# Splitting four of W_out's eight row blocks in the second half's narrow projection groups, and loading them as parts at attention's end

## The chip, the cores and the metric

One core of one Trainium2 chip runs the kernel. The metric is device time in microseconds (us). The kernel has engines with queues of their own, each of which runs its instructions in order: TensorE (PE; its weight loads are listed as PEld), VectorE (DVE), ScalarE (ACT), GpSimd (POOL) and SyncE (SP). SP does no arithmetic and issues most DMA transfers; POOL and ACT can issue DMAs too. Sixteen DMA engines serve all queues.

## The reference

One decoder layer on 2048 tokens of width 1024, in float32: an RMSNorm, one input projection, two mixers (gated linear attention, GLA, and dilated sliding-window attention), an output projection, then an MLP. What matters here is the output projection, which takes the GLA heads' 512 columns (after their own norm, with its gain `gla_norm_g`) and the attention heads' 512 columns through one matrix of 1024 x 1024:

```python
o_a = o_a * lax.rsqrt(jnp.mean(o_a * o_a, axis=-1, keepdims=True) + EPS)
o_a = o_a * gla_norm_g[l].astype(jnp.float32).reshape(GLA_HEADS, GLA_DV)
o_a = o_a.reshape(B, S, GLA_WIDTH) * jax.nn.silu(gr.astype(jnp.float32))
...
mixed = jnp.concatenate([o_a, o_b], axis=-1).astype(h.dtype)
h = h + jnp.einsum('bsm,md->bsd', mixed, w_out[l])
```

## The kernel before

A product in float32 precision is made of three TensorE products of parts (`mm3`, L139 to L142): each operand is *split* into a rounded part hi, which ScalarE writes, and the rest lo, which VectorE writes. So every matrix that takes part has to be split somewhere, at a cost of one ScalarE and one VectorE operation for each piece.

The kernel runs in stages: the input projection (to about 476 us), attention with GLA beside it (to about 855 us), the output projection W_out with the norm (to about 1035 us), then the MLP.

*Input projection.* The tokens are taken in two halves, and in each half nine groups of W_in's columns are gone through (`groups`), numbered g = 0 to 8 and, in the second half, NG = 9 to 17. A group has seven jobs (`jobs`), the seven products of a Strassen-like scheme. The *narrow* groups, g = 11 to 16 in the second half, have 128 columns; their jobs have the order 1, 2, 6, 5, 7, 3, 4 (`linked`), and each is twelve products of 128x512, some 2.7 us. `prep(at + 2)` splits the weights of the job after next (ScalarE L304, VectorE L306, or L308 where a scale goes in) and adds them up in place (VectorE L310 to L316). `load_w` fetches the next group's raw weights (`wraw`), on SP's queue, or on POOL's for the last group. L310 is the first operation that needs a group's new weights. The order of instructions written out in this part ends with the first half. From there on a planner, at compile time, gives each engine its order from a model of the costs; `tc.keep_in_program_order` pins one instruction behind all that its engine was given so far.

*SBUF.* All large tiles come from one ring of 25 slots (`slot`, L127). A tile that wants a slot waits until an earlier tile is done with, and a DMA into it waits on its queue.

*Attention.* The loop goes by units of score blocks: scores (L930, L932), VectorE's bias and minimum (L940), ScalarE's exponential (L941), transposes (L950), the copy of the transposed block to `pt` by ScalarE (L957) or VectorE (L959) in turns, products with v (L969). GLA's steps run between them (L1093 to L1165; L1107 copies the scores under a mask, L1160 needs what it copied, L1153 is an exponential). Other work is hung on unit numbers by `at_unit`. One such work is `load_wo`: in the last units, every third unit, one of W_out's eight rows of blocks c (128 rows each) is loaded whole, 0.5 MB, into `woraw` (SP, L1188). Rows 0 to 3, GLA's, are multiplied by the norm's gain `gn` and split into the blocks 1 (left half) and 12 (right half), in tiles `wb` (ScalarE L1193, VectorE L1194). Rows 4 to 7 are split whole into tiles `wo` (L543, L544, in the helper `split`). The rows go in the order 4, 0, 1, 5, 2, 3, 6, 7. Each `wb` tile holds two rows' pieces of one block, hi and lo.

*Output projection.* It reads the parts by `wo_part`, the first products after 853 us. Further blocks (4 to 7) are sums of these; their sums were made earlier in attention by `sum_wo` on POOL, stored to `wtD`, and are loaded and split by `mix_wo`.

The main lines of `load_wo`:

```python
c = (4, 0, 1, 5, 2, 3, 6, 7)[len(loaded)]
...
raw = slot("woraw")[:, :D]
SP.dma_start(raw, wo[:, c])
```

Of the kernel before, what the change touches and what calls it, by code (L numbers as in the profile page):

```python
# [18 lines left out]
D = 1024  # L19
# [10 lines left out]
AHEAD, LAG = 3, 2  # L30
# [84 lines left out]
def emit(tc, a, stop=99):  # L115
    nc = tc.nc
    V, A, G, T, SP = nc.vector, nc.scalar, nc.gpsimd, nc.tensor, nc.sync
# [4 lines left out]
    dram = es.enter_context(tc.tile_pool(name="dram", bufs=1, space=bass.MemoryType.DRAM))  # L122

    def ps(tag):
        return psum.tile([128, 512], F32, name="ps_" + tag, tag=tag, bufs=BANKS[tag])

    def slot(name, dt=F32, n=SLOT):  # L127

        return up.tile([128, SLOT], dt, name=name, tag="u", bufs=25)[:, :n]

    def view(t, shape):
        n = int(np.prod(shape))
        names = "abcd"[:len(shape)]
        return t[:, :n].rearrange(f"p ({' '.join(names)}) -> p {' '.join(names)}", **dict(zip(names, shape)))
# [27 lines left out]
    gn = stats[:, 44:]  # L162
    stat_at = [0]

    def stat(n=1):
        if stat_at[0] + n > 44:
            stat_at[0] = 0
        s = stats[:, stat_at[0]:stat_at[0] + n]
        stat_at[0] += n
        return s  # L170

    def rstd_of(ssq, width, n=1, bias=eps):
        r = stat(n)
        A.activation(r, ssq, AF.Ln, bias=bias, scale=1.0 / width)
        A.activation(r, r, AF.Exp, scale=-0.5)
        return r
# [75 lines left out]
    NG = len(groups)  # L252
# [3 lines left out]
    jobs = [(g, j) for g in range(2 * NG) for j in (linked if chained(g) else order)]  # L256
# [263 lines left out]
    def bias_rows():  # L520

        rb, oh, rbo = xp[:33, :8], view(xp[:33, 8:], (3, 384)), view(bp[:8], (3, 384))
        SP.dma_start(rb[:32], a["rel_bias"])
        SP.dma_start(oh, a["c_onehot"])
        V.memset(rb[32:33], NEG)
        yield
        V.tensor_scalar(rb[:32], rb[:32], -1.0, None, op0=OP.mult)
        for d in range(3):
            p = ps("d")
            T.matmul(p[:8, :384], rb, oh[:, d], start=True, stop=True)  # L530
            V.tensor_copy(rbo[:, d], p[:8, :384])
        SP.dma_start(rowD, rbo)
        yield
# [8 lines left out]
    def split(hi, lo, src):  # L542
        A.activation(hi, src, AF.Copy)  # L543
        V.tensor_tensor(lo, src, hi.bitcast(F32), op=OP.subtract)  # L544

    def x_load(t, dst):
        SP.dma_start(dst, x2[t * 128:t * 128 + 128])
# [13 lines left out]
    def transposed(xt, last=None, pin=False, by=ident):  # L561
        out = []
        for q in range(2):
            pv = view(ps("cd"[q]), (4, 128))
            for k in range(4):
                of = xt[:, (4 * q + k) * 128:(4 * q + k + 1) * 128]
                ins = T.transpose(pv[:, k, :], last if last is not None and 4 * q + k == 7 else of, by)
                if pin and q + k == 0:
                    tc.keep_in_program_order(ins)
            out.append(pv)  # L570
        return out
# [33 lines left out]
    def second_half():  # L605

        b = [view(bp[:, 512 * q:], (4, 128)) for q in range(4)]
        for i in range(4):
            for k in range(2):
                x_load(8 + 4 * k + i, xp[:, D * k:D * k + D])  # L610
            yield
            for k in range(2):
                xt = xp[:, D * k:D * k + D]
                ss = stat()
                tc.keep_in_program_order(A.activation(bp[:, :D], xt, AF.Square, accum_out=ss))
                r = rstd_of(ss, D)
                V.scalar_tensor_tensor(xt, xt, r, gB, op0=OP.mult, op1=OP.mult)
            yield
            for k in range(2):
                for q, pv in enumerate(transposed(xp[:, D * k:], pin=True, by=perm)):  # L620
                    A.activation(b[2 * k + q], pv, AF.Copy)
                yield
            (b11, b21, b12, b22), (t2, t4, t3) = b, [view(xp[:, 512 * q:], (4, 128)) for q in range(3)]
            V.tensor_tensor(b12, b12, b11, op=OP.subtract)
            V.tensor_tensor(t2, b22, b12, op=OP.subtract)
            for j, v in ((2, b21), (1, b11), (5, b12), (6, t2), (3, b22), (4, t4), (7, t3)):
                if j == 5:
                    yield
                    V.tensor_tensor(t4, b21, t2, op=OP.subtract)
                    V.tensor_tensor(t3, t2, b11, op=OP.subtract)  # L630
                SP.dma_start(nTD[j - 1][:, :, i * 128:i * 128 + 128], v)
            yield
# [21 lines left out]
    def reload(n):  # L654

        j, cs = order[n // 2], slice(1024 * (n % 2), 1024 * (n % 2) + 1024)
        t = (xp, bp)[n // 2 % 2][:, cs]
        SP.dma_start(t, nTD[j - 1].rearrange("p c s -> p (c s)")[:, cs])

        def rest():  # L660
            hi, lo = [v[:, cs] for v in TF[j]]
            tc.keep_in_program_order(A.activation(hi, t, AF.Copy))
            V.tensor_tensor(lo, t, hi.bitcast(F32), op=OP.subtract)
            if n + 4 < 14:
                back.append(reload(n + 4))

        return rest

    with tc.manual_schedule(engines={nc.tensor.engine, nc.vector.engine, nc.scalar.engine, nc.gpsimd.engine}):
# [19 lines left out]
        w = view(first_w[0][0], (2, 4, 256))  # L689
# [108 lines left out]
    SP.dma_start(w2b[33:50].bitcast(F32), w2raw[33:].bitcast(F32))  # L798
    for gT in gTs:
        A.activation(gT, ident, AF.Copy, scale=0.0)  # L800
    other, back, bias = second_half(), [], bias_rows()
    for at in range(7, len(jobs)):
        g = jobs[at][0]
        prep(at + 2)
        if at in (7 * NG - 7, 7 * NG - 6):
            back.extend(reload(2 * (at - 7 * NG + 7) + k) for k in range(2))
        for i in range(4 if groups[g % NG][2] > 128 else 1):
            ready = gated[:]
            product(at, i)()
            for t in ready:  # L810
                gate_product(t)
                gated.remove(t)
        if behind and chained(g):
            f, *args = behind.pop(0)
            f(*args)
        if back and at >= 7 * NG - 5:
            back.pop(0)()
            back.pop(0)()
        if at in OTHER:
            next(other)  # L820
        if at == len(jobs) - 14:
            heads = load_head(0)
        if at in (len(jobs) - 13, len(jobs) - 10, len(jobs) - 9):
            next(heads)
        if at in (7 * NG + 3, 7 * NG + 5):
            next(bias)
        if 7 * NG + 8 <= at < 7 * NG + 44 and at % 3 == 0:
            spread_bias(2 - (at - 7 * NG - 8) // 12, (at - 7 * NG - 8) // 3 % 4 * 2)
# [336 lines left out]
                    A.activation(st[:, j], st[:, j], AF.Copy, scale=w[:, j:j + 1])  # L1165
                yield

    wo = a["w_out"].rearrange("o (c p) n -> p (o c) n", p=128)
    WO, WB, loaded = {}, {}, []

    def block_view(j, c):

        if (j, c // 2) not in WB:
            WB[j, c // 2] = view(slot(f"wb{j}", FR), (2, 2, 512))
        return [WB[j, c // 2][:, c % 2, i] for i in range(2)]

    def wo_part(j, c):

        if j in (2, 3):
            return [WO[c][:, i, 512 * (j - 2):512 * (j - 2) + 512] for i in range(2)]  # L1180
        return block_view(j, c)

    def load_wo(n):
        for _ in range(n):
            c = (4, 0, 1, 5, 2, 3, 6, 7)[len(loaded)]
            loaded.append(c)
            raw = slot("woraw")[:, :D]
            SP.dma_start(raw, wo[:, c])  # L1188
            if c < 4:
                for j, n in ((1, 0), (12, 1)):  # L1190
                    hi, lo = block_view(j, c)
                    r = raw[:, 512 * n:512 * n + 512]
                    A.activation(hi, r, AF.Copy, scale=gn[:, c:c + 1])  # L1193
                    V.scalar_tensor_tensor(lo, r, gn[:, c:c + 1], hi.bitcast(F32), op0=OP.mult, op1=OP.subtract)  # L1194
            else:
                w = WO[c - 4] = view(slot("wo", FR), (2, D))
                split(w[:, 0], w[:, 1], raw)

    wtD = dram.tile([4, 128, 2 * D], F32, name="wtD")

# [56 lines left out]
    def at_unit(n, *f):  # L1257
        plan.setdefault(n, []).append(f)
# [16 lines left out]
    for pr in range(4):  # L1275
# [3 lines left out]
        for hh, br in seq:  # L1279
# [7 lines left out]
            if br == 2 and first:  # L1287
                pieces = load_head(b.h)
# [15 lines left out]
    NU = len(units)  # L1304
# [1 line left out]
    for n, x in enumerate(sums_wo):  # L1306
        at_unit(8 + AHEAD + n, next, x)
    for i in range(8):
        at_unit(NU - 28 + 3 * i + AHEAD, load_wo, 1)
    gla = gla_steps()  # L1310
    for k in range(-AHEAD, NU + LAG):
        tr, pv, sc = iter(()), iter(()), iter(())
# [314 lines left out]
    for at in range(4):  # L1627
        p, e = divmod(at, 2)
# [31 lines left out]
    for g in range(14, 56):  # L1660
        p, i = divmod(g, 7)
# [161 lines left out]
    for at in range(len(jobs1)):  # L1823
# [7 lines left out]
        n = at + 6 - len(jobs1)  # L1831
# [15 lines left out]
    for ph, (_, chained, _, _) in enumerate(PRODUCTS):  # L1847
# [3 lines left out]
        for k in range(4):  # L1851
            n = 4 * ph + k
# [76 lines left out]
```

## Time and profile before

| | us |
|---|---|
| median of 3 runs | 2239.28 |
| lowest and highest | 2235.93, 2239.9 |
| the profiled execution | 2235.3 |
| its span, first to last instruction | 2233.5 |
| share of PE, DVE, ACT, POOL busy in the span | 99%, 74%, 55%, 24% |

How to read the lines that follow. A row of the *timeline* has the start and the length in us, the engine, the line of the code, the operation, what it writes <- what it reads, the shape, and in brackets the idle time of the engine before it with what ended that. A row of the *waits* names who waited <- for what: us in total, times, longest. A row of the *groups* ends with: busy time, mean ns of one | idle time before, with what ended most of it. A row of the *DMA issues* has how many, KB each, and the median us from issue to landing. A row of the *windows* gives a stretch of time, its length, then the busy time (and instructions) of PE, PEld, DVE, ACT and POOL, the clock that TensorE was granted (1.00 is full speed), the busy share of the DMA engines, and GB/s. DMA times are on SP's queue where a row says SPq. A matmul's end is modelled, so TensorE's busy time isn't the same as TensorE at its peak.

### The profile page before, as it was taken

To read this page: it belongs to the slowest core of one execution; us is meant where nothing else is said; L and a number is where in the kernel's file an instruction comes from. 1 tells how busy PE (TensorE), PEld (TensorE's weight loads), DVE (VectorE), ACT (ScalarE), POOL (GpSimd) and SP (SyncE) were. 2 spreads that over 40 slices of the span, in tenths; PEclk is the share of its full clock that TensorE was granted. 3 is DMA by queue.
4 is the path that set the end of the run, shared out by engine and by line. 5 is a ranking of instruction groups with operands and counts; after the bars stand their busy time and mean duration, and the time that the engine had idled before them with its cause. 6 is when DMAs were issued, how large, how long until landed. Compare 5 with 4: busy or idle time off the path is not lost.

```text
span 2233.5 us, 34965 instructions
## 1 busy us (share of the span) xinstructions
PE 2208.3 (99%) x12420; PEld 1918.8 (86%) x12420; DVE 1650.9 (74%) x3093; ACT 1236.2 (55%) x2420; POOL 528.4 (24%) x527
## 2 busy tenths in 40 slices
PE   9999999999999999999999999999999999999998
PEld 8988998899999988887788887888888888888877
DVE  8676766657777788778776788777686697576798
ACT  7365524437888885546555566555555433333446
POOL 1000000026586673000000000000007222042462
PEclk9999999999999999999999999999999999999999
DMA  6566855677967966768644456555489998677775
GB/s 208 176 216 190 268 152 170 208 216 260 322 226 238 278 199 245 239 227 269 208 147 142 140 178 192 158 174 161 130 287 284 307 295 270 216 247 253 253 258 197
DMA packets 331763, 491.50 MB, mean 220 GB/s; under 512 B 20615, under 2 KB 225050, under 8 KB 320836
## 3 DMA queue, kind: packets, MB, share of 16 engines
q1 hardware_dynamic: 307282, 381.97, 52.7%
q0 software_dynamic: 16960, 54.60, 9.7%
q10 hardware_dynamic: 7346, 52.70, 6.2%
q8 instruction: 98, 1.61, 0.3%
q14 instruction: 77, 0.63, 0.1%
HBM read 335.25 MB, written 158.66 MB: 221 GB/s over the span
## 4 chain that ended last, share of the span: by engine, by line
PE 75%; issue 16%; DMA 3%; DVE 3%; POOL 2%; ACT 1%; POOLq 0%; ACTq 0%; SPq 0%; DVEq 0%
PE ps_a L141 8%; PE ps_a L142 8%; PE ps_a L140 8%; PE ps_c L141 6%; PE ps_c L142 6%; PE ps_c L140 6%; PE ps_a L969 4%; PE ps_d L141 4%; PE ps_d L142 4%; PE ps_d L140 4%; PE ps_o L140 3%; PE ps_o L141 3%; PE ps_o L142 3%; PE ps_d L950 3%; PE ps_c L932 2%
## 5 line engine op out<-in xcount | busy, mean ns | idle before, releaser
L543 ACT ACTIVATE cb<-bs 128x1024 fp32r<-128x1024 f32 x104 | 110.1, 1060 | 286.4 <-PE ps_c L141 95.4
L544 DVE TENSOR_TENSOR cb<-bs,cb 128x1024 fp32r<-128x1024 f32 x104 | 161.5, 1553 | 136.8 <-ACT cb L543 136.4
L1749 POOL TENSOR_TENSOR bs<-bs,rb 128x1024 f32<-128x1024 f32 x60 | 173.9, 2904 | 312.8 <-DMA bs<-w_ff 280.8
L544 DVE TENSOR_TENSOR w1comb<-w1raw,w1comb 128x512 fp32r<-128x512 f32 x224 | 153.5, 687 | 92.5 <-ACT w1comb L543 92.4
L1456 POOL DMA_DIRECT2D w1raw<-w_ff x64 | 48.1, 752 | 701.4 <-DVE w1comb L544 524.9
L543 ACT ACTIVATE w1comb<-w1raw 128x512 fp32r<-128x512 f32 x224 | 139.8, 627 | 89.1 <-PE ps_c L142 26.1
L969 PE MATMUL ps_a<-v,pt 128*128 128x65 f32 x1200 | 178.6, 253 | 1.8 <-ACT pt L957 1.8
L969 PEld LDWEIGHTS ps_a<-v,pt 128*128 128x128 f32 x1200 | 173.9, 195 | 3.8 <-ACT pt L957 2.7
L941 ACT ACTIVATE pe<-pe,O 128x256 f32<-128x256 f32 (+1 forms) x384 | 154.9, 453 | 13.5 <-DVE O L940 12.3
L950 PE MATMUL ps_d<-ident,pe 128*128 128x128 f32 x600 | 159.5, 280 | 1.2 <-ACT pt L957 1.1
L304 ACT ACTIVATE wcomb<-wraw 128x512 fp32r<-128x512 f32 (+2 forms) x119 | 90.4, 759 | 114.4 <-PE ps_a L141 54.6
L940 DVE CUSTOM_DVE_ANT_0 pe<-ps_c,nb 128x256 f32<-128x256 f32 (+1 forms) x384 | 125.7, 360 | 34.3 <-PE ps_d L950 23.0
L140 PE MATMUL ps_c<-hb,w1comb 128*128 128x512 f32 x320 | 124.6, 390 | 0.8 <-DVE acc L1545 0.8
L141 PE MATMUL ps_c<-hb,w1comb 128*128 128x512 f32 x320 | 124.5, 389 | 0.0
L142 PE MATMUL ps_c<-hb,w1comb 128*128 128x512 f32 x320 | 124.0, 389 | 0.0
L141 PE MATMUL ps_c<-cb,ca 128*128 128x512 f32 x312 | 121.4, 389 | 0.0
L142 PE MATMUL ps_c<-cb,ca 128*128 128x512 f32 x312 | 121.4, 389 | 0.0
L140 PE MATMUL ps_c<-cb,ca 128*128 128x512 f32 x312 | 121.4, 389 | 0.0
L544 DVE TENSOR_TENSOR ca<-ra,ca 128x1024 fp32r<-128x1024 f32 x84 | 119.7, 1426 | 0.1
L306 DVE TENSOR_TENSOR wcomb<-wraw,wcomb 128x512 fp32r<-128x512 f32 (+2 forms) x77 | 73.2, 950 | 53.3 <-ACT wcomb L304 53.2
L950 PEld LDWEIGHTS ps_d<-ident,pe 128*128 128x128 f32 x600 | 108.6, 186 | 1.7 <-ACT pt L957 1.3
L1530 ACT ACTIVATE acc<-acc 128x512 f32<-128x512 f32 x96 | 60.6, 632 | 68.3 <-DVE acc L1549 31.7
(490 smaller groups left out, 7174.4 us busy)
## 6 DMA issues: line engine op xcount, KB each, us to landing
ra<-actD ACTq DMA_DIRECT2D x50, 1024.0 KB, 7.4
actD<-ring SPq DMA_DIRECT2D x176, 256.0 KB, 3.0
rb<-w_ff SPq DMA_DIRECT2D x88, 512.0 KB, 5.9
bs<-w_ff SPq DMA_DIRECT2D x72, 512.0 KB, 6.6
w1raw<-w_ff POOLq DMA_DIRECT2D x64, 512.0 KB, 5.5
k<-kD SPq DMA_DIRECT2D x16, 1024.0 KB, 9.0
rb<-hTD SPq DMA_DIRECT2D x28, 512.0 KB, 5.0
wraw<-w_in SPq DMA_DIRECT2D x48, 256.0 KB, 3.7
```

The lines of the kernel that those rows point to most:

```text
L140: T.matmul(out, sh, mh, start=first, stop=False, **kw)
L141: T.matmul(out, sl, mh, start=False, stop=False, **kw)
L142: T.matmul(out, sh, ml, start=False, stop=last, **kw)
L304: A.activation(hi, src, AF.Copy, scale=sc)
L306: V.tensor_tensor(lo, src, hi.bitcast(F32), op=OP.subtract)
L543: A.activation(hi, src, AF.Copy)
L544: V.tensor_tensor(lo, src, hi.bitcast(F32), op=OP.subtract)
L940: V.tensor_tensor_reduce(p, s, bias, scale=1.0, scalar=BIG, op0=OP.add, op1=OP.min, accum_out=nm)
L941: A.activation(p, p, AF.Exp, bias=nm, scale=-1.0)
L950: T.transpose(pb[:, i * 128:i * 128 + 128], src, ident)
L969: T.matmul(self.b.opsum[:, n % 4], self.pt[:, i * 128:i * 128 + 128], self.b.v[:, blk, cols], start=first, stop=last)
L1749: (engines or ((G,), (V, V))[len(sums) - 1])[e].tensor_tensor(v, v, r, op=OP.add if op == "+" else OP.subtract)
```

## The change

Rows 0 to 3 of W_out are no longer loaded and split at attention's end. In the second half of the input projection a new generator, `split_wo`, takes two slots (`wsum` for two raw rows, `wsplit` for parts). At the job with index 4 of group 11 POOL issues the loads of rows 0 and 1. After job 6 (the third job) of each of the groups 12 to 15 one row is taken: two ScalarE operations (hi, with the gain), two VectorE operations (lo) and, on POOL's queue, two stores of 0.5 MB to the new DRAM tiles `wsD`, for block 1 and for block 12; after rows 0 and 1 POOL also loads rows 2 and 3. At attention's end the places of rows 0 to 3 in `load_wo` are taken by four loads of ready parts (`load_parts`), 1 MB each, straight into `wb` tiles on SP's queue: (block 1, rows 0 and 1), (block 12, rows 0 and 1), and the same with rows 2 and 3. Rows 4 to 7 are loaded and split as before, and all eight places keep their units.

```diff
+    wo = a["w_out"].rearrange("o (c p) n -> p (o c) n", p=128)
+    wsD = {j: dram.tile([2, 128, 2, 2, 512], F32, name=f"wsD{j}") for j in (1, 12)}
+
+    def split_wo():
+
+        raw, pieces = view(slot("wsum"), (2, D)), view(slot("wsplit", FR), (2, 2, 512))
+        for c in range(2):
+            G.dma_start(raw[:, c], wo[:, c])
+        yield
+        for n in range(8):
+            c, h = divmod(n, 2)
+            p = pieces[:, h]
+            r = raw[:, c % 2, 512 * h:512 * h + 512]
+            w = gn[:, c:c + 1] if c < 4 else 1.0
+            tc.keep_in_program_order(A.activation(p[:, 0], r, AF.Copy, scale=w))
+            V.scalar_tensor_tensor(p[:, 1], r, w, p[:, 0].bitcast(F32), op0=OP.mult, op1=OP.subtract)
+            G.dma_start(wsD[((1, 12), (2, 3))[c // 4][h]][c % 4 // 2, :, c % 2], p.bitcast(F32))
+            if h and c < 2:
+                G.dma_start(raw[:, c % 2], wo[:, c + 2])
+            yield
+
+    of_wo = split_wo()
...
+        if at == 7 * NG + 18:
+            next(of_wo)
+        if NG + 3 <= g < NG + 7 and jobs[at][1] in (6,):
+            for _ in range(2):
+                next(of_wo)
...
+    def load_parts(j, h):
+
+        t = slot(f"wb{j}", FR, 2048)
+        WB[j, h] = view(t, (2, 2, 512))
+        SP.dma_start(t.bitcast(F32), wsD[j][h].rearrange("p c i n -> p (c i n)"))
+
...
-    def load_wo(n):
-        for _ in range(n):
-            c = (4, 0, 1, 5, 2, 3, 6, 7)[len(loaded)]
-            loaded.append(c)
+    def load_wo(c):
+        if isinstance(c, tuple):
+            load_parts(*c)
+        else:
             raw = slot("woraw")[:, :D]
             SP.dma_start(raw, wo[:, c])
-            if c < 4:
-                for j, n in ((1, 0), (12, 1)):
-                    hi, lo = block_view(j, c)
-                    r = raw[:, 512 * n:512 * n + 512]
-                    A.activation(hi, r, AF.Copy, scale=gn[:, c:c + 1])
-                    V.scalar_tensor_tensor(lo, r, gn[:, c:c + 1], hi.bitcast(F32), op0=OP.mult, op1=OP.subtract)
-            else:
-                w = WO[c - 4] = view(slot("wo", FR), (2, D))
-                split(w[:, 0], w[:, 1], raw)
+            w = WO[c - 4] = view(slot("wo", FR), (2, D))
+            split(w[:, 0], w[:, 1], raw)
...
-        at_unit(NU - 28 + 3 * i + AHEAD, load_wo, 1)
+        at_unit(NU - 28 + 3 * i + AHEAD, load_wo, (4, (1, 0), (12, 0), 5, (1, 1), (12, 1), 6, 7)[i])
```

More of the change, by code (lines that the diff above doesn't have):

```diff
@@ L1166, in gla_steps @@
                 yield
-    wo = a["w_out"].rearrange("o (c p) n -> p (o c) n", p=128)
-    WO, WB, loaded = {}, {}, []
+    WO, WB = {}, {}
     def block_view(j, c):
```

## The prediction

> **What bounds the kernel now.** I read the page's busy times first.
>
> ```profile
> PE 2208.3 (99%) x12420; PEld 1918.8 (86%) x12420; DVE 1650.9 (74%) x3093; ACT 1236.2 (55%) x2420; POOL 528.4 (24%) x527
> ```
>
> TensorE is idle for 2233.5 - 2208.3 = 25 us in all. No edit of other engines' work can save more than the idle time, and what a slower clock adds, in the stages that it touches. So I asked who makes TensorE wait around the end of attention, from 802 to 862 us.
>
> ```profile
> PE ps_a L969 <- ACT pt L957: 1.6, 1, 1.6
> PE ps_o L1160 <- DVE gla L1107: 1.5, 1, 1.5
> PE ps_c L1439 <- DVE O L940: 1.4, 1, 1.4
> PE ps_d L950 <- ACT pt L957: 1.1, 1, 1.1
> ```
>
> Four stalls, 5.6 us, in the stretch where W_out's rows are loaded and split. The stretches of 20 us from 800 on show how full the helpers are there:
>
> ```profile
> 800.00:820.00 20.00, 16.77 (x123) 15.25 (x123) 16.87 (x55) 14.27 (x39) 16.88 (x25) 0.85 0.70 232
> 820.00:840.00 20.00, 18.95 (x173) 18.64 (x172) 17.51 (x56) 18.79 (x53) 11.88 (x18) 0.98 0.77 235
> 840.00:860.00 20.00, 18.59 (x152) 17.35 (x152) 17.98 (x40) 14.43 (x39) 16.25 (x26) 1.00 0.89 318
> ```
>
> After the length come the busy times of PE, PEld, DVE, ACT and POOL, then PE's clock, the DMA share and the rate. VectorE and ScalarE are near full, and the clock drops. The timelines of ScalarE, VectorE and TensorE show how the stalls come about:
>
> ```profile
> 810.23 1.34 ACT L1193 ACTIVATE wb<-woraw,stats 128x512 fp32r<-128x512 f32 x2 [1.71 <-DMA woraw<-w_out]
> ...
> 813.50 1.06 ACT L543 ACTIVATE wo<-woraw 128x1024 fp32r<-128x1024 f32 x1 [1.84 <-DMA woraw<-w_out]
> 814.47 1.26 ACT L1153 ACTIVATE gla<-gla,stats 128x128 f32<-128x128 f32 x4
> 815.63 0.57 ACT L957 ACTIVATE pt<-ps_d 128x512 f32<-128x512 f32 x1
> ```
>
> ```profile
> 810.99 0.75 DVE L1194 SCALAR_TENSOR_TENSOR wb<-woraw,stats,wb 128x512 fp32r<-128x512 f32 x1 [2.36 <-ACT wb L1193]
> 811.66 0.72 DVE L1107 COPY_PREDICATED gla<-gla,ps_o 128x512 f32<-128x512 int32 x1
> ```
>
> ```profile
> 812.43 1.13 PE L1160 MATMUL ps_o<-gla 128*128 128x256 f32 x4 [1.48 <-DVE gla L1107]
> ...
> 816.26 1.97 PE L969 MATMUL ps_a<-v,pt 128*128 128x65 f32 x8 [1.62 <-ACT pt L957]
> ...
> 825.28 0.66 PE L950 MATMUL ps_d<-ident,pe 128*128 128x128 f32 x4 [1.05 <-ACT pt L957]
> ```
>
> The first stall is the change's own subject: row 1's load lands late, ScalarE's split L1193 waits 1.71 us for it in line, VectorE's L1194 waits behind that, L1107 behind L1194, and TensorE behind L1107. The second has another row: ScalarE waits 1.84 us for row 5's load at L543, which the change keeps, and L957 stands behind it.
>
> The half-speed clock that goes with them:
>
> ```profile
> 814.20:816.30 2.10, 0.48 (x4) 0.19 (x2) 2.10 (x7) 2.10 (x7) 2.10 (x3) 0.50 1.05 408
> 816.30:820.90 4.60, 4.60 (x22) 4.60 (x23) 3.79 (x13) 2.27 (x7) 4.60 (x4) 0.50 0.46 148
> ```
>
> TensorE did 0.48 + 4.60 = 5.1 us of work at 0.50, which at full clock takes half: 2.5 us lost.
>
> **The change part by part.** *Removed at attention's end:* the eight splits of rows 0 to 3.
>
> ```profile
> L1193 ACT ACTIVATE wb<-woraw,stats 128x512 fp32r<-128x512 f32 x8 | 5.5, 715 | 1.7 <-DMA woraw<-w_out 1.7
> ```
>
> ```profile
> L1194 DVE SCALAR_TENSOR_TENSOR wb<-woraw,stats,wb 128x512 fp32r<-128x512 f32 x8 | 7.6, 955 | 4.1 <-ACT wb L1193 4.1
> ```
>
> That is 5.5 us of ScalarE and 7.6 us of VectorE, and a place where both wait on a DMA. None of it is on TensorE, so it is worth only stalls. I go through them. The first (1.48 us) loses its cause: taken whole. The third (1.05) ends when a busy ScalarE comes to L957, and L1193 is part of what it does before that: taken whole. The second (1.62) stays on row 5's load. That load leaves SP after a slot comes free:
>
> ```profile
> SPq L1188 <- DMA boD<-O: 1.6, 1, 1.6
> ```
>
> Four raw rows fewer pass through the ring of slots, so I take half of the stall, 0.8. Of the fourth (1.4, a VectorE that is 17.98 of 20 busy) I also take half, 0.7, since 7.6 us of VectorE work leaves the stage before it. The half clock came with two stalls close together; with one of them gone I take its 2.5 us as saved. Sum: 1.48 + 1.05 + 0.8 + 0.7 + 2.5 = 6.5 us. The ends are 0 (every stall finds another cause) and 5.6 + 2.5 = 8.1.
>
> On the clock there is a rule that speaks against this. The Trainium skill (TensorE: Matmul & The Clock Gate, Part 1: The HAM clock gate) says that the gate judges free-running windows of about 3.4 us, and that an idle one closes it to half and a busy one opens it. This trace agrees: half clock from about 814 to 820.9 us is two such windows. By it the second stall, if it stays, can hold the gate closed for one window by itself, an estimate of 1.7 us lost, and the saving would be 4.8 and not 6.5.
>
> *Added at attention's end:* four loads of 1 MB in place of four of 0.5 MB (the raw rows):
>
> ```profile
> woraw<-w_out SPq DMA_DIRECT2D x8, 512.0 KB, 3.8
> ```
>
> 2.1 MB more, at the 318 GB/s of the 840 to 860 stretch 6.6 us of DMA time over some 45 us. The parts are read only when the first W_out products start after 853 us, so they themselves hide; what they delay in SP's queue is row 5's load, GLA's and those of the mixed rows. At nothing in the sum; its price if uncovered is the second rival.
>
> *Added in the second half's narrow groups:* eight ScalarE and eight VectorE operations, two in each group after job 6. VectorE's own of that shape takes 0.69 us there, less than the 955 ns above, as POOL does nothing beside it:
>
> ```profile
> L308 DVE SCALAR_TENSOR_TENSOR wcomb<-wraw,wcomb 128x512 fp32r<-128x512 f32 x14 | 9.6, 688 | 8.3 <-ACT wcomb L304 8.3
> ```
>
> ```profile
> 374.40:393.50 19.10, 19.10 (x88) 15.67 (x87) 12.79 (x24) 11.56 (x27) 0.00 (x0) 1.00 0.73 200
> 393.50:412.60 19.10, 19.10 (x86) 15.82 (x85) 10.66 (x17) 9.29 (x14) 0.00 (x0) 1.00 0.80 234
> ```
>
> These are the first two groups concerned. 1.4 us more on each of two engines that are busy 13 us of 19 or less is covered by the products. If it weren't, it would cost at most 4 x 1.4 = 5.6 us. The twelve DMA issues go to POOL, busy 0.00 there, past nothing; its next loads, for the last group, stand behind the last store and have most of a group's time. The raw loads precede their first use by five jobs of 2.7 us.
>
> What has no cover is the transfers' time. They are 4 loads and 8 stores of 0.5 MB, 1.5 MB in each of the first two groups and 1 MB in the others, and SP's loads of w_in run beside them. VectorE waits for those already, in its timeline:
>
> ```profile
> 391.44 0.69 DVE L310 TENSOR_TENSOR wraw<-wraw 128x512 f32<-128x512 f32 x1 [1.88 <-DMA wraw<-w_in]
> ...
> 394.19 0.68 DVE L308 SCALAR_TENSOR_TENSOR wcomb<-wraw,wcomb 128x512 fp32r<-128x512 f32 x1
> ...
> 412.50 0.69 DVE L310 TENSOR_TENSOR wraw<-wraw 128x512 f32<-128x512 f32 x1 [3.46 <-DMA wraw<-w_in]
> ```
>
> and TensorE's timeline shows when it needs what stands behind L310, the split for job 2:
>
> ```profile
> 396.31 0.39 PE L140 MATMUL ps_c<-tb,wcomb 128*128 128x512 f32 x1
> ```
>
> ```profile
> 416.00 0.50 PE L141 MATMUL ps_c<-tb,wcomb 128*128 128x512 f32 x1 [0.27 <-DVE wcomb L306]
> ```
>
> The slack is 396.31 - 394.87 = 1.4 us in the first group and nothing in the second. So a later landing is a stall at once. Around the second one the DMA engines stand thus:
>
> ```profile
> 404.00:410.50 6.50, 6.50 (x30) 5.39 (x29) 2.56 (x4) 3.10 (x5) 0.00 (x0) 1.00 0.99 314
> 410.50:412.60 2.10, 2.10 (x11) 1.74 (x10) 0.10 (x1) 0.29 (x1) 0.00 (x0) 1.00 0.04 8
> ```
>
> Full until 410.5, then empty until the landing is told. Two stores (1.05 MB at 314 GB/s) are 3.3 us of this; if all of it comes ahead of w_in's last piece, the stall is 3.3 in the second group. The lower end is 0: L310 isn't needed for another group, and the planner, which places it afresh, may put it behind the split. Upper end: the raw loads as well, 5.0 us for each of the first two groups. I take 1.0 for all, near the lower end, since it is the row of one group alone that has no slack.
>
> Sum: -6.5 + 1.0 = -5.5 us. The profiled execution took 2235.3 us (span 2233.5), 4.0 below the median of 2239.28, and would take 2229.8; from the median, 2233.8.
>
> **The rivals.** *The stores hold up w_in (slower).* Place: L310 in the narrow groups. For it: the full DMA engines, the missing slack. Price: 3.3 - 1.4 = 1.9 in the first group, 3.3 in the second, 1.9 (slack as in the first) in the third, none in the fourth, whose successors load later; 7.1, and 2.5 if stalls longer than the 1.48 above again bring half clock: 9.6. It decides once the second half loses more than the 6.5 gained. With the gain kept it ends at +3.1; with half of it kept and both raw loads in the way (+3.4), at +9.7. Between: +6, 2245. Against it: the planner's freedom.
> The Trainium skill speaks for it (DMA: Bandwidth & Descriptors, Queues, rings and completion order): each DMA engine takes turns between the queues that have work, packet by packet, so POOL's queue gets its share beside SP's. No row here shows POOL and SP traffic in these groups together; by that rule the outcome is this rival's 2245.
>
> *The wait moves to row 5 (no change).* Its load now follows 1 MB where 0.5 MB stood; 0.52 MB at 314 GB/s is 1.7 us, so L543 starts 1.7 later, takes up the first stall's 1.48, and the clock stays down. Left are 1.05 + 0.7 - 0.2 - 1.0 = 0.5 us: 2238.8. For it: L543 waits 1.84 already. Against: the 1.6 us that SP waited for a slot.
>
> **How the numbers follow.** Forecast 0.45, first rival 0.38, second 0.17. Some 0.2% (4.5 us) is about what a measurement of this kernel can tell from no change. The forecast's own range is 2231 (all 8.1 us) to 2237; four fifths of it is faster by more than 0.2%: 0.36. No change: the rest of it and three quarters of the second rival, 0.22. Slower: 0.42, the first rival and what is left. The range over all is 2231 to 2247; beyond it lie the first rival's end at 2249 and a gain larger than the stalls.
>
> **What would show it.** Right: no split from woraw into wb after 780 us, TensorE's waits from 802 to 862 at 3 us or less, the clock at 1.00 from 800 to 840, L310's waits as before. The first rival: L310 waiting 5 us or more for w_in and a TensorE stall on L306 or L308 in two groups. The second: ScalarE's L543 waiting 3 us or more with the stall on L957 behind it. Wrong altogether: an end that moves by other stages, the MLP above all, which this change doesn't touch.

## The result and the profile after

| us | before | after |
|---|---|---|
| median of 22 runs each | 2237.43 | 2234.49 |
| lowest and highest | 2232.8, 2241.98 | 2229.27, 2238.83 |
| the profiled execution | 2235.3 | 2234.55 |
| its span | 2233.5 | 2232.8 |

The ratio of after to before is 0.9984, with a 95% interval of 0.9977 to 0.9991: about 3 us are won, 0.16%. That is inside the 0.2% which the prediction called no change, though the interval keeps off 1. The forecast had 5.5 us. Its time, 2233.8, is within 0.7 us of the 2234.49 measured, but that is luck: it counted from 2239.28, the median of 3 runs of the kernel before, and over 22 runs that median is 2237.43.

The span can be cut at two places that both kernels have: attention's first scores and the first product with W_out. The timeline of TensorE, after:

```profile
513.55 0.23 PE L957 MATMUL ps_c<-k,qp 128*128 128x128 f32 x1
...
852.58 0.48 PE L140 MATMUL ps_d<-wb,mT 128*128 128x512 f32 x1
```

and before:

```profile
510.81 0.23 PE L930 MATMUL ps_c<-k,qp 128*128 128x128 f32 x1
...
853.76 0.48 PE L140 MATMUL ps_d<-wb,mT 128*128 128x512 f32 x1
```

So the second half of the input projection lost 513.55 - 510.81 = 2.74 us, and attention became 342.95 - 339.03 = 3.92 us shorter. Two terms of opposite sign, both larger than the 1.2 us that is left of them. Each profile is one execution: these two are 0.75 us apart, where the medians are 2.9 apart.

**Attention's end.** TensorE's waits from 802 to 862 us, after, then the stretches of 20 us (the columns are those of the prediction's windows):

```profile
PE ps_a L996 <- ACT pt L984: 2.7, 3, 1.4
PE ps_a L996 <- DVE O L999: 0.3, 1, 0.3
```

```profile
800.00:820.00 20.00, 18.25 (x157) 17.20 (x157) 16.79 (x54) 14.57 (x43) 17.12 (x26) 1.00 0.88 308
820.00:840.00 20.00, 20.00 (x186) 19.69 (x185) 17.00 (x63) 18.38 (x54) 13.89 (x24) 1.00 0.94 310
840.00:860.00 20.00, 18.76 (x141) 16.82 (x141) 17.00 (x41) 11.38 (x33) 16.28 (x22) 1.00 0.81 291
```

The stalls there went from 5.6 to 3.0 us, and the clock (the third number from the end) is 1.00 throughout. The stall behind GLA's L1107 (L1134 now) is gone. What stays is the wait for row 5: ScalarE's timeline, and TensorE's with the largest of the three stalls left:

```profile
815.84 1.06 ACT L543 ACTIVATE wo<-woraw 128x1024 fp32r<-128x1024 f32 x1 [2.07 <-DMA woraw<-w_out]
```

```profile
817.43 1.11 PE L996 MATMUL ps_a<-v,pt 128*128 128x65 f32 x8 [1.42 <-ACT pt L984]
```

**The second half.** VectorE's timeline around the second of the four groups that split, and TensorE's:

```profile
394.87 0.69 DVE L310 TENSOR_TENSOR wraw<-wraw 128x512 f32<-128x512 f32 x1 [3.26 <-DMA kD<-acc]
...
403.52 1.42 DVE L816 SCALAR_TENSOR_TENSOR wsplit<-wsum,stats,wsplit 128x512 fp32r<-128x512 f32 x2 [0.94 <-ACT wsplit L815]
...
417.52 0.69 DVE L310 TENSOR_TENSOR wraw<-wraw 128x512 f32<-128x512 f32 x1 [6.18 <-DMA wraw<-w_in]
418.13 0.68 DVE L306 TENSOR_TENSOR wcomb<-wraw,wcomb 128x512 fp32r<-128x512 f32 x1
...
435.59 0.69 DVE L310 TENSOR_TENSOR wraw<-wraw 128x512 f32<-128x512 f32 x1 [2.27 <-DMA wraw<-w_in]
```

```profile
418.87 0.50 PE L141 MATMUL ps_c<-tb,wcomb 128*128 128x512 f32 x1 [3.22 <-DVE wcomb L306]
```

VectorE stands 6.18 us at the add L310 (3.46 before), behind it waits the split L306, and TensorE waits 3.22 us for that split. It is the only stall of the kind. The DMA engines in these microseconds:

```profile
404.00:410.50 6.50, 6.50 (x30) 5.38 (x29) 5.31 (x9) 3.79 (x7) 1.59 (x3) 1.00 1.09 354
410.50:413.00 2.50, 2.50 (x13) 2.07 (x12) 0.84 (x1) 0.87 (x3) 0.00 (x0) 1.00 1.06 257
413.00:417.50 4.50, 2.65 (x12) 1.88 (x10) 0.00 (x0) 2.57 (x4) 0.00 (x0) 1.00 1.02 352
```

Where they stood empty from 410.5 before, they are full until the piece has landed at 417.5. VectorE does nothing at all from 413.0 to 417.5.

### The profile page after: what moved, and what is told of

It is laid out like the page before. It is cut to its first block, busy times and chain, and to the rows that moved or that the text cites. A ratio compares the mean times of both kernels' runs of the same rounds, so it can differ in the third digit from the quotient of the medians.

```text
span 2232.8 us, 35003 instructions
## 1 busy us (share of the span) xinstructions
PE 2206.5 (99%) x12420; PEld 1917.5 (86%) x12420; DVE 1646.0 (74%) x3093; ACT 1237.1 (55%) x2420; POOL 535.5 (24%) x539
## 4 chain that ended last, share of the span: by engine, by line
PE 77%; issue 15%; DMA 3%; DVE 2%; POOL 2%; ACT 1%; SPq 0%; POOLq 0%; ACTq 0%; DVEq 0%
PE ps_a L141 8%; PE ps_a L142 8%; PE ps_a L140 8%; PE ps_c L141 6%; PE ps_c L142 6%; PE ps_c L140 6%; PE ps_a L996 4%; PE ps_d L141 4%; PE ps_d L142 4%; PE ps_d L140 4%; PE ps_o L140 3%; PE ps_o L141 3%; PE ps_o L142 3%; PE ps_d L977 3%; PE ps_c L959 2%
## 5 line engine op out<-in xcount | busy, mean ns | idle before, releaser
L543 ACT ACTIVATE cb<-bs 128x1024 fp32r<-128x1024 f32 x104 | 110.2, 1060 | 285.3 <-PE ps_c L141 92.0
L543 ACT ACTIVATE w1comb<-w1raw 128x512 fp32r<-128x512 f32 x224 | 139.9, 627 | 89.7 <-PE ps_c L142 26.4
L141 PE MATMUL ps_c<-hb,w1comb 128*128 128x512 f32 x320 | 124.4, 389 | 0.0
L141 PE MATMUL ps_c<-cb,ca 128*128 128x512 f32 x312 | 121.4, 389 | 0.0
L306 DVE TENSOR_TENSOR wcomb<-wraw,wcomb 128x512 fp32r<-128x512 f32 (+2 forms) x77 | 73.1, 949 | 48.1 <-ACT wcomb L304 48.0
```

The lines of the kernel that those rows point to most:

```text
L141: T.matmul(out, sl, mh, start=False, stop=False, **kw)
```

## The experiments

My theory was the sum above: a gain at attention's end, and a loss in one place, at L310, which the planner puts so early that VectorE stands in line for weights that are wanted only a group later. Eleven runs tested it. The table has, from each one's profile, the start of the first scores, the time from there to the first product with W_out, L310's longest wait in groups 11 to 16; then the median less that of the kernel before on the same chip, and the ratio. The ratio isn't the quotient of the two medians, and the two columns can differ by up to 0.07%.

| kernel | first scores | to W_out | L310 | median | ratio, 95% interval |
|---|---|---|---|---|---|
| before | 510.81 | 342.95 | 3.46 | | |
| after | 513.55 | 339.03 | 6.18 | -2.9 | 0.9984, 0.9977 to 0.9991 |
| E1 split alone | 511.80 | 345.33 | 5.00 | +3.2 | 1.0013, 0.9999 to 1.0026 |
| E2 parts alone | 509.87 | 338.84 | 2.43 | -3.3 | 0.9978, 0.9966 to 0.9990 |
| E3 after, L310 pinned | 510.55 | 339.15 | none | -5.0 | 0.9975, 0.9964 to 0.9986 |
| E4 before, L310 pinned | 509.48 | 347.78 | none | +1.4 | 1.0004, 0.9993 to 1.0015 |
| E5 after job 3 | 514.68 | 339.12 | 4.79 | -1.5 | 0.9993, 0.9980 to 1.0006 |
| E6 stored twice | 515.35 | 338.15 | 5.21 | +0.7 | 1.0003, 0.9991 to 1.0015 |
| E7 pinned, row 5 sooner | 509.53 | 340.18 | none | -5.5 | 0.9979, 0.9967 to 0.9991 |
| E8 split, not stored | 509.78 | 341.63 | 3.36 | -4.6 | 0.9976, 0.9964 to 0.9988 |
| E9 stored twice, pinned | 509.65 | 338.46 | none | -7.9 | 0.9967, 0.9954 to 0.9980 |
| E10 after, again | 513.34 | 339.25 | 5.13 | -2.8 | 0.9991, 0.9979 to 1.0004 |
| E11 after, L310 pinned, again | 510.10 | 339.86 | none | -8.5 | 0.9962, 0.9947 to 0.9978 |

**E1, the split alone.** The kernel before, with `split_wo` and its two calls in the second half; attention's end keeps the eight splits.

```diff
+    of_wo = split_wo()
...
+        if at == 7 * NG + 18:
+            next(of_wo)
+        if NG + 3 <= g < NG + 7 and jobs[at][1] in (6,):
+            for _ in range(2):
+                next(of_wo)
```

> The kernel before, plus the second half's part of the change: the raw rows of W_out, their splits and the four pairs of stores. The attention's end is as before, and the stored halves are read by nobody. My theory (the second half lost the whole gap): attention's first scores move from 510.8 to 513 to 514 us, one wait of TensorE of about 3 us stands in the second group with splits, behind the add at L310, and the run is 2 to 4 us over the kernel before (ratio 1.001 to 1.0018). The rival (the two halves of the change only act together, or the shift is the scheduler's scatter): first scores within 1 us of 510.8 and a ratio within 0.0005 of 1.

The ratio is as expected, 1.0013, though its interval just touches 1. The stall is there, but smaller, 2.0 us and not 3; VectorE's and TensorE's timelines:

```profile
415.81 0.69 DVE L310 TENSOR_TENSOR wraw<-wraw 128x512 f32<-128x512 f32 x1 [5.00 <-DMA wraw<-w_in]
```

```profile
417.15 0.50 PE L141 MATMUL ps_c<-tb,wcomb 128*128 128x512 f32 x1 [2.03 <-DVE wcomb L306]
```

The first scores come at 511.80, so only 1.0 us after those of before; the expected 513 was missed, and the rival's "within 1 us" is just met. It is E8 and E3 below that decide between the two. The stall needs nothing of attention's end to come about.

**E2, the parts alone.** The changed kernel without `split_wo`:

```diff
-        SP.dma_start(t.bitcast(F32), wsD[j][h].rearrange("p c i n -> p (c i n)"))
+        SP.dma_start(t.bitcast(F32), nTD[2 * h + j // 12].rearrange("p c s -> p (c s)"))
```

> The changed kernel without the split in the second half: the four loads of parts at attention's end read stretches of the same form and size, 1 MB each, from another stored array, so that W_out's blocks 1 and 12 of rows 0 to 3 are other numbers. My theory (attention's end gained about 4 us and this is its whole gain): first scores within 1 us of 510.8, the first product with W_out at 849 to 850 us, and 4 to 6 us under the kernel before (ratio 0.9973 to 0.9982). The rival (the gain at attention's end is partly the queue having been in another state after a later start): first product at 852 to 853.8 and a ratio of 0.999 to 1.

First scores at 509.87, first product with W_out at 848.71, ratio 0.9978: the gain at attention's end is real by itself, and it needs no late start. L310 waits 2.43 us at most. By the medians E2 is 3.3 us under the kernel before, less than the 4 to 6 expected; the ratio lies in the expected range. E1's and E2's ratios together make -0.0009; after's -0.0016 and E10's -0.0009 lie there too.

**E3 and E4, L310 pinned.** The same three lines in the changed kernel and in the one before:

```diff
-            V.tensor_tensor(a21, a21, a22, op=OP.add)
+            ins = V.tensor_tensor(a21, a21, a22, op=OP.add)
+            if g >= NG:
+                tc.keep_in_program_order(ins)
```

> The changed kernel, with the add at L310 kept in the order in which the program has it in the second half, so that VectorE does not meet it before the products' copies that the program issues first. My theory (the add, put a whole group early, blocks VectorE while w_in's last piece is late): no TensorE wait of 3 us in that group, first scores at 510.3 to 511.3 us, 3 us under the changed kernel, so a ratio of 0.9968 to 0.9976 to the kernel before. The rival (the work added to VectorE and ScalarE itself delays the group, or the late piece is wanted by the product itself): the wait stays at 2.5 us or more, ratio 0.998 to 0.999.

> The kernel before, with the same add at L310 kept in the program's order in the second half. My theory: before, the piece that L310 waits for lands some 5 us earlier, so there is little to win: first scores within 0.5 us of 510.8, ratio 0.9994 to 1.0003. The rival (the order of L310 is worth 3 us whatever the stores do): first scores at 508, ratio 0.9985 to 0.999.

VectorE's timeline of E3, at the same place and a group later:

```profile
411.57 0.69 DVE L306 TENSOR_TENSOR wcomb<-wraw,wcomb 128x512 fp32r<-128x512 f32 x1
412.17 0.69 DVE L310 TENSOR_TENSOR wraw<-wraw 128x512 f32<-128x512 f32 x1
...
449.95 0.69 DVE L310 TENSOR_TENSOR wraw<-wraw 128x512 f32<-128x512 f32 x1
```

No add has a wait in brackets, the split goes first, and the last narrow group's add runs at 449.95, where the changed kernel had it at 435.59: the planner had indeed moved each of these adds about a group ahead. TensorE has no stall at L141 in the second half, the first scores are back at 510.55, and the ratio is 0.9975. With the splits and the stores left in, only the order of one VectorE operation gives back what the second half lost; so the rival, that the added work itself takes the time, is out. Pinned in the kernel before, the same lines win nothing that can be measured (1.0004), so it isn't what the planner changes around the pin either. E4's first scores are 1.3 us earlier than before's, more than expected; E2 and E8, which have no pin, are as early, so that much is scatter between builds.

**E5, the same at another job.**

```diff
-        if NG + 3 <= g < NG + 7 and jobs[at][1] in (6,):
+        if NG + 3 <= g < NG + 7 and jobs[at][1] in (3,):
```

> The changed kernel with the splits and stores of the second half put after each group's third job in place of its sixth. My theory (the cost is a store sharing the DMA engines with a piece of w_in that an add put early waits for): the stores are issued some 7 us sooner in the group, while pieces of w_in are rarer, so L310's idle time behind wraw is under 3 us in every group and TensorE's stall there under 1 us; first scores at 510 to 511.5 us, ratio to the kernel before 0.9972 to 0.998. The rival (the added work of VectorE and ScalarE costs the time, wherever it stands): a stall of 2 to 4 us in one group as before, first scores at 513 or later, ratio 0.998 to 0.999.

A miss, and the edit doesn't do what was expected of it: the jobs run 1, 2, 6, 5, 7, 3, 4, so job 3 is the sixth of a group and job 6 the third. The stores come later and not 7 us sooner: the first pair is issued at 396.79 us, where the changed kernel has 384.66. L310 waits in two groups now, and TensorE has four stalls of 0.6 to 1.1 us, 3.5 in all:

```profile
414.86 0.69 DVE L310 TENSOR_TENSOR wraw<-wraw 128x512 f32<-128x512 f32 x1 [3.74 <-DMA wraw<-w_in]
...
436.02 0.69 DVE L310 TENSOR_TENSOR wraw<-wraw 128x512 f32<-128x512 f32 x1 [4.79 <-DMA wraw<-w_in]
```

From the new place, too, there is a piece of w_in that L310 waits for. The 3.5 us of stalls and first scores at 514.68 are nearer to the rival's numbers than to mine; E3 and E8 keep it from being the rival's cause. The run doesn't test an earlier place, and how the piece comes to be late here isn't shown.

**E8, split but not stored.** The changed kernel without the stores of line 817, the parts loaded as in E2.

```diff
-            G.dma_start(wsD[((1, 12), (2, 3))[c // 4][h]][c % 4 // 2, :, c % 2], p.bitcast(F32))
```

> The changed kernel with the raw rows' loads and the splits of the second half left as they are, but the halves not stored; attention's end loads stretches of the same size and form from another stored array, so that W_out's blocks 1 and 12 of rows 0 to 3 are other numbers. My theory (the stores, with the raw load between them, delay w_in's piece): without the stores the piece lands 3 to 4 us sooner, TensorE's stall at L141 in the second group is under 1 us, first scores at 510 to 511.5 us, ratio 0.9970 to 0.998. The rival (the splits on VectorE and ScalarE delay the group): stall 2 to 3.2 us, first scores at 512.5 or later, ratio 0.998 to 0.999.

```profile
412.70 0.69 DVE L310 TENSOR_TENSOR wraw<-wraw 128x512 f32<-128x512 f32 x1 [3.36 <-DMA wraw<-w_in]
```

```profile
PE ps_c L141 <- DVE wcomb L306: 0.4, 1, 0.4
```

All operations of ScalarE and VectorE and the raw loads are there, the stores are not, and L310's wait is 3.36 as it was before (3.46), the stall 0.4 us. The stores make the wait.

**E6 and E9, every store made twice,** into a second array; E9 has the pin besides.

```diff
             G.dma_start(wsD[((1, 12), (2, 3))[c // 4][h]][c % 4 // 2, :, c % 2], p.bitcast(F32))
+            G.dma_start(wsE[((1, 12), (2, 3))[c // 4][h]][c % 4 // 2, :, c % 2], p.bitcast(F32))
```

> The changed kernel with each store of a split half made twice, to a second array too, so 8 MB of stores in place of 4 and the same work on every engine. My theory: w_in's last piece lands a further 2 to 4 us later in each of the four groups, L310's longest idle time goes from 6.2 to 8 to 10 us, TensorE's stalls in the second half from 3.2 to 6 to 12 us in all, first scores at 516 to 522 us, ratio to the kernel before 1.0000 to 1.0035. The rival (the engines' added work costs the time, not the stores): first scores within 1 us of 513.5, ratio 0.998 to 0.999.

> The changed kernel with every store of a split half made twice, as in the earlier run, and with the add at L310 kept in the program's order. My theory (a late piece of w_in costs only because L310, wanted a group later, waits for it in VectorE's line): even with 8 MB of stores L310 waits for nothing or under 1 us, TensorE's stalls in the second half are under 1 us (3.9 without the pin), first scores at 509.5 to 511 us (515.35 without), ratio to the kernel before 0.9970 to 0.9985. The rival (the DMA engines themselves are too full, so that the piece is late for its product too): stalls of 2 to 4 us stay, first scores at 513 or later, ratio 0.9990 to 1.0005.

E6's loss grew less than expected: first scores at 515.35 and not 516 to 522, two stalls of 2.3 and 1.6 us, L310's longest wait 5.21 and not 8 to 10, ratio 1.0003. In the second group the planner put L310 one split later than in the changed kernel (L306 runs at 412.35, ahead of it), so the 2.3 us fall on the next job's product. How late the piece lands can be read from SP's queue, where w_in's last two pieces of the group are issued, and from L310's start on VectorE. Before, without stores, then after, E1, E8 and E6; the rows of L310 that stand already aren't shown again:

```profile
404.25 3.04 SPq L284 DMA_DIRECT2D wraw<-w_in  x2
```

```profile
405.57 1.65 SPq L284 DMA_DIRECT2D wraw<-w_in  x2
```

```profile
405.02 1.68 SPq L284 DMA_DIRECT2D wraw<-w_in  x2
```

```profile
404.50 1.68 SPq L284 DMA_DIRECT2D wraw<-w_in  x2
```

```profile
406.67 1.66 SPq L284 DMA_DIRECT2D wraw<-w_in  x2
...
419.57 0.69 DVE L310 TENSOR_TENSOR wraw<-wraw 128x512 f32<-128x512 f32 x1 [5.20 <-DMA wraw<-w_in]
```

From the end of the issue to the landing it takes 412.50 - 407.29 = 5.2 us before, 412.70 - 406.18 = 6.5 with the raw load alone, 417.52 - 407.22 = 10.3 with two stores, and 419.57 - 408.33 = 11.2 with four. E1 and E10, with two stores as well, have 415.81 - 406.70 = 9.1 and 415.78 - 406.54 = 9.2, so some 1 us is scatter. The first two stores cost 2.6 to 3.8 us, two more 0.9 to 2.1, though 1.05 MB at the 352 GB/s above are 3.0 us of DMA time, and all four are issued by 407.78, before SP's own issue ends at 408.33. So the piece seems not to stand behind all that POOL has issued, as far as one profile with four stores can show it. The Trainium skill (DMA: Bandwidth & Descriptors, Queues, rings and completion order) says that each DMA engine goes round the queues that have work, a packet at a time; a deeper POOL queue then takes no larger share from SP's. These traces agree with it, within their scatter: 0.9 to 2.1 us where 3.0 would be the full price.

E9 settles the matter. With twice the stores, the pin alone takes the first scores from 515.35 to 509.65, L310 waits nowhere, and the kernel is 0.9967 of before. The full DMA engines cost nothing where nobody stands in line for what they carry.

**E7, row 5 sooner,** with the pin:

```diff
-        at_unit(NU - 28 + 3 * i + AHEAD, load_wo, (4, (1, 0), (12, 0), 5, (1, 1), (12, 1), 6, 7)[i])
+        at_unit(NU - 28 + 3 * i + AHEAD, load_wo, (4, (1, 0), 5, (12, 0), (1, 1), (12, 1), 6, 7)[i])
```

> The changed kernel with the add at L310 kept in the program's order (as in the run before with that pin) and, at attention's end, row 5 of W_out loaded one unit group ahead of the part (block 12, rows 0 and 1), where the changed kernel loads that part first. My theory (the stalls left at 813 to 817 us come from ScalarE waiting in line for row 5): ScalarE's wait behind woraw for row 5 is under 0.3 us, TensorE's stalls after the exponentials fall by 1 to 1.7 us in all, first product with W_out 338 us or less after attention's first scores (339.0 in the changed kernel), ratio 0.9966 to 0.9973. The rival (the slot that woraw is read into comes free late, so the load is no sooner for being asked for sooner; or the wait goes to another row): the first product stays 339 to 340 us after the first scores, ratio 0.9973 to 0.998.

The wait for row 5 is gone, and with it the stalls behind ScalarE's copies to `pt`. ScalarE's and TensorE's timelines:

```profile
806.31 1.05 ACT L545 ACTIVATE wo<-woraw 128x1024 fp32r<-128x1024 f32 x1
```

```profile
807.99 1.02 PE L1135 MATMUL ps_o<-gla 128*128 128x256 f32 x4
...
811.14 0.39 PE L959 MATMUL ps_c<-k,qs 128*128 128x256 f32 x1 [2.13 <-DVE O L969]
```

and VectorE's, with the windows of the same stretch:

```profile
809.16 0.29 DVE L969 CUSTOM_DVE_ANT_0 pe<-ps_c,nb 128x128 f32<-128x128 f32 x1 [3.53 <-PE ps_o L1135]
```

```profile
808.00:811.50 3.50, 1.37 (x9) 0.92 (x8) 2.33 (x8) 2.30 (x9) 2.94 (x5) 1.00 0.89 236
811.50:815.00 3.50, 3.50 (x22) 3.50 (x21) 2.64 (x10) 2.82 (x10) 1.57 (x6) 0.51 1.05 370
```

VectorE now stands 3.53 us at L969 until a GLA product (L1135) has run, TensorE stalls 2.13 us for the scores behind it, and the clock goes to half after that. Attention took 340.18 us, no less than after's 339.03, and the ratio, 0.9979, is in the rival's range. The wait went elsewhere, as the rival said; why VectorE came to stand just there wasn't followed further.

**E10 and E11, after and its pinned version once more, on one chip.**

> The changed kernel itself, beside the next run on one chip. From its first comparison: ratio 0.9977 to 0.9991 to the kernel before, first scores at 513 to 514 us.

> The changed kernel with the add at L310 kept in the program's order, beside the changed kernel on one chip. My theory: 2 to 3 us under the changed kernel, ratio 0.9965 to 0.9980 to the kernel before. The rival (the first comparison of the two was scatter between chips): the two medians within 1 us.

Medians of 2235.55 and 2229.81: the pinned version is 5.7 us under the changed kernel here, more than the 2 to 3 expected, where the two earlier comparisons differ by 2.0. Both are above zero; the intervals of E10 and E11 don't meet, those of the earlier two overlap. E10's ratio is at the end of its expected range, E11's is 0.9962. So the change with L310 pinned is under the kernel before in both comparisons, by 5.0 and 8.5 us, and under the changed kernel clearly in one. The profiles don't explain the 5.7 us: at the first scores E11 is 3.2 us ahead (513.34 to 510.10), but its profiled execution took 2235.8 us, 6.0 above its own median, and its MLP 1196.7 us against E10's 1193.9.

## Why the prediction was right, and where it was not

The direction, the two places and the signs at attention's end came true, and the time lies in the range; by the prediction's own band of 0.2%, though, the outcome is no change, to which it gave 0.22.

**The gain at attention's end** was put at 6.5 us and came out at 3.9 between the two profiles. Stall by stall: the first (1.48) and the third (1.05) are gone, as said. Of the second, half was to go; it stayed, 1.62 to 1.42, since row 5's load came no sooner (L543 waits 2.07 us for it, 1.84 before). Of the fourth 0.7 was to be left, and two stalls of 0.65 and 0.59 us stand there behind the copies to `pt`. So the stalls gave 2.6 where 4.0 had been summed. With the clock's 2.5 that would still be 5.1; a stall of 1.08 us at 535 us, where before has one of 0.64 at 570, takes back 0.4 of it, and the rest of the way to 3.9 isn't accounted for.

The clock stayed at 1.00 from 800 to 860, as said, though the second stall stayed: the Trainium skill's rule (TensorE: Matmul & The Clock Gate, Part 1: The HAM clock gate) had given an estimate of 1.7 us lost to that stall alone, which the clock of 1.00 in these rows doesn't bear out. That is luck in part. By the borders of the clock's windows that the last section works out, the second stall of after (816.01 to 817.43) is cut at 816.46 into 0.45 and 0.97 us, while the first stall of before (810.95 to 812.43) lies whole in the window that ends at 814.04, where its half speed begins.

The pair isn't the whole measure, however. Three profiles have the raw rows at attention's end (before, E1, E4): 342.95, 345.33 and 347.78 us from the first scores to W_out, mean 345.4. Nine have the parts in after's order: 338.15 to 341.63, mean 339.3. That is a gain of 6.1 us, and the profile of before was the luckiest of its kind. But E4's profiled execution was the slowest of its twelve (2242.31, median 2238.41); without it the gain is 4.9. The medians lie between: the five kernels with the parts in after's order and no loss in the second half (E2, E3, E8, E9, E11) are 3.3 to 8.5 us under the kernel before, 5.8 in the mean. E4's rows show the bad kind of luck:

```profile
800.00:820.00 20.00, 16.49 (x126) 15.11 (x125) 16.93 (x52) 14.27 (x39) 16.93 (x25) 0.91 0.72 229
820.00:840.00 20.00, 19.42 (x166) 19.12 (x166) 17.57 (x55) 18.00 (x49) 10.95 (x14) 0.92 0.71 208
840.00:860.00 20.00, 17.80 (x143) 16.87 (x142) 14.97 (x38) 14.59 (x40) 13.19 (x26) 0.91 0.94 333
```

The clock falls below 1.00 in all three stretches. Half speed lasts 6.8, 3.4 and 10.2 us of attention's end in before, E1 and E4, and 3.4 us in two of the nine others (E2 and E5): with half of that lost, the change saves 3.0 us in the mean, near the 2.5 of the prediction. The stalls' part in the term was too high, then, and the clock's part depends on which execution it is read from.

**The step that failed is the term of 1.0 us for the transfers in the second half.** It measured 2.7 us at the first scores of the pair; over three kernels with the stores after job 6 and no pin (after, E1, E10: mean 512.9) against eight without stores or with the pin (mean 510.0) it is 2.9. The mechanism and its place were in the prediction: the landing of w_in's last piece, L310, the second group without slack, at 3.3 us. It was then priced near its lower end, because the planner "may put it behind the split". The planner did put it three operations later in VectorE's line, but still ahead of the split. The piece was as late as the upper end said: 417.52 against 412.50 is 5.0 us. With 2.9 in place of 1.0 and 4.9 to 6.1 in place of 6.5 the sum is -2.0 to -3.2, against -2.9 measured.

**The first rival** named what happened, but counted it in three groups, at 7.1 us. It came in one, 3.2 us. Of its signs, L310 waiting 5 us or more is there (6.18), a stall in two groups isn't. In the first group L310 ran 3.4 us later than before (394.87 against 391.44; its row names a store of kD as what came last) and TensorE lost nothing by it: the planner had put three operations ahead of L310 that stood behind it before, and the split behind it ended at 396.17, in time for the product L141 at 396.41. So the freedom that the prediction counted on helped there. No half clock came with the stall in after's profile (E10's, further down, has it). **The second rival** is seen in part: row 5's wait stayed, 2.07 us, less than the 3 that would have shown it, and it didn't take up the first stall.

The eight splits in the second half were costed at nothing, and E8 and E3 show that they cost nothing. That the four loads of 1 MB hide themselves is borne out too: no wait of TensorE ends on them.

**The MLP,** which the change doesn't touch, gave back 0.6 us (1193.5 us from its first product to the last, 1192.9 before). At its start, the timeline of TensorE after, then before:

```profile
1037.67 0.50 PE L140 MATMUL ps_d<-hb,w1comb 128*128 128x512 f32 x1 [2.49 <-ACT w1comb L543]
```

```profile
1038.04 0.50 PE L140 MATMUL ps_d<-hb,w1comb 128*128 128x512 f32 x1 [1.50 <-ACT w1comb L543]
```

The stage starts 1.4 us sooner and waits 1.0 longer for its weights; in after the clock drops behind that:

```profile
1038.30:1041.80 3.50, 3.50 (x10) 2.76 (x9) 3.50 (x7) 2.35 (x6) 0.00 (x0) 0.51 0.78 274
```
Over all profiles the MLP takes 1190.3 to 1196.7 us without any order in it that goes with the edits, so nothing is read from it. That spread is twice the change's effect, which is why single executions here can't show a difference of 3 us in the whole time.

## What to carry to other kernels

When transfers are added beside others, look for the operation that stands in line for a load that nobody needs yet: it turns a late landing into a stall of everything behind it, and pinning that one operation was worth as much as the whole loss, with the transfers left in, even doubled. Where a profile shows no slack behind such an operation, price the stall in full and not near nothing in the hope that a planner will move it. A term made of stalls and clock drops in one execution should be read from several profiles where there are some: here its size went from 3.9 us in one pair to 4.9 or 6.1 in the mean of eleven or twelve profiles.

## What the runs showed of the hardware that was not expected

The length of a stall alone doesn't decide whether the clock drops. In E10 a stall of 2.16 us is followed by half speed; the rows are TensorE's timeline and windows:

```profile
417.13 0.50 PE L141 MATMUL ps_c<-tb,wcomb 128*128 128x512 f32 x1 [2.16 <-DVE wcomb L306]
```

```profile
414.40:417.80 3.40, 1.24 (x6) 0.73 (x5) 2.02 (x4) 1.12 (x2) 0.00 (x0) 1.00 0.38 136
417.80:421.30 3.50, 3.50 (x10) 2.75 (x9) 3.31 (x5) 0.00 (x0) 0.00 (x0) 0.51 0.65 183
```

After's stall at the same product is 3.22 us long and leaves the clock at full speed:

```profile
413.69:417.10 3.41, 1.96 (x9) 1.30 (x7) 0.00 (x0) 1.88 (x4) 0.00 (x0) 1.00 1.06 358
417.10:420.52 3.42, 1.65 (x7) 1.38 (x8) 3.00 (x5) 0.00 (x0) 0.00 (x0) 1.00 0.12 45
```

and in E2 one of 1.59 us was enough:

```profile
839.95 0.44 PE L970 MATMUL ps_a<-v,pt 128*128 128x65 f32 x2 [1.59 <-ACT pt L958]
```

```profile
837.00:840.90 3.90, 2.31 (x21) 1.99 (x20) 3.56 (x8) 3.60 (x9) 3.82 (x2) 1.00 0.13 47
840.90:844.40 3.50, 3.50 (x22) 3.50 (x21) 1.95 (x7) 3.12 (x13) 1.62 (x2) 0.51 0.92 312
```

The Trainium skill (TensorE: Matmul & The Clock Gate, Part 1: The HAM clock gate) has the gate judge windows that run freely, whatever the work does; a stall across the border of two such windows then counts for less in each. The traces agree. Read from windows of 0.5 us, the half-speed stretches start at 417.82 and 1039.04 us in E10, at 840.92 and 1035.48 in E2, and at 811.53, 1036.81 and 2146.15 in E7: 182, 57, 66 and 325 times 3.413 us apart, and each lasts 3.4 us. Before's one stretch, from 814.04 to 820.87, is twice that.

After's only stretch starts at 1038.33. 182 steps back lies a border at 417.10, inside its stall (415.65 to 418.87): 1.45 us come before it and 1.77 behind, in the two windows whose rows stand above. E10's 2.16 us (414.97 to 417.13) lie whole between the borders at 414.41 and 417.82, and E2's 1.59 between 837.51 and 840.92. How much idle time in one window is enough isn't a single number here: E6's stall of 1.60 us (395.79 to 397.39) lies whole between 395.06 and 398.48, and its clock stays up, while E2's 1.59 among attention's smaller products was enough. What makes that difference stays open.
